# An encoder layer with neighbourhood attention and a gated scan: level scores on four column tiles in two runs per block, and second query copies by DMA

## The chip, the core and the metric

The kernel runs on one core of a Trainium2 chip. The metric is the device time of one execution in microseconds. Engine names are those of the profile: PE is TensorE (PEld its weight loads), DVE is VectorE, ACT is ScalarE, POOL is GpSimd and SP is SyncE; POOL and SP here mostly issue DMAs.

## What is computed

One encoder layer over 2048 tokens (a grid of 32 rows by 64 columns) with 1024 features, in float32. One input projection feeds an attention of 8 heads over a clamped 8 x 16 window with a learned bias, and a gated linear scan of 4 heads in both directions; both results are gated, concatenated, projected and normalised.

```python
h = jnp.einsum('btd,de->bte', x, w_in) + b_in
q_a, k_a, v_a, g_a, q_h, z_fwd, z_bwd, i_h, g_h = jnp.split(h, split_at, axis=-1)
o_a = neighbourhood_attention(heads_a(q_a), heads_a(k_a), heads_a(v_a), rpb) * jax.nn.silu(g_a)
# scan, per direction: S_t = diag(f_t) S_{t-1} + k_t outer v_t,  o_t = S_t^T q_t
o_fwd = hgrn2_chunk_scan(qh, k_f, ih, logf_f)
o_bwd = flip(hgrn2_chunk_scan(flip(qh), flip(k_b), flip(ih), flip(logf_b)))
o_h = rms_norm(o_fwd + o_bwd) * hg_norm_gain * jax.nn.silu(g_h)
y = jnp.einsum('bte,ed->btd', jnp.concatenate([o_a, o_h], axis=-1), w_out) + b_out
out = layer_norm(DEEPNORM_ALPHA * x + y)
```

## The kernel before, in words

Tokens are worked on in four blocks of 512, in two halves of two blocks. A half has four scan units (`hg_unit`, one head each) and four attention units (`att_unit`, two heads each). The input projection (`projections`) is written as a generator that issues one 128x512 matmul at a time: PE records `pj`, and `pv` for the two wide value projections. These are the **fillers**. Each unit is a generator as well, and yields weights; the driver at the end of `_build` spreads the fillers of a unit (between two entries of `marks`) over these weights. `in_order` (behind `mm` and `transpose`) ties TensorE's instructions to the order in which the code issues them, so TensorE's order is written by hand: unit work, some fillers, unit work. The other engines' instructions are ordered by a scheduler, roughly by the order of the code, with `tc.high_priority` moving some ahead. Float32 operands of the big projections are split into two float32r parts, a rounded one (a cast on ScalarE) and the rest (a subtraction on VectorE).

**A scan block** (`hg_phase1`, 16 in all: four heads, four token blocks) works by levels. In each chunk of 128 tokens it needs a 128x128 score matrix `A`. The diagonal comes from `ks` and `q`; the pairs at distance level 1, 2, 4, 8, 16, 32 each from a pair of mixed operands `km` and `qm` (in buffers named km, qm, ub or kt, copied by ScalarE at L502 and L504); level 64, the off-diagonal halves, from `ST` itself. Between levels VectorE multiplies running products into `ST` (L513, L514) and halves the products (`PX`, L516). The scores are held until the last level and then all issued in one run (`visit`, PE records `plev`): 64 matmuls with 64 output columns and 64 moving columns, which write the upper or lower 64 partitions of four PSUM banks. `collect` puts them together: a multiply by an identity (L481) and predicated copies with a mask per level (L483) into `AH`, which holds the two diagonal 64x64 blocks, then four copies into `A` (L485 to L488). Then follow the transposes `pk`, the state updates `pu` and `pub`, and the outputs `po`.

**An attention unit** goes through groups of 8 token rows; a group has four items, one per column window. `prep_q` splits a query tile for both heads into `hi` and `lo`, each of which is needed in both halves of the partitions: four casts on ScalarE and four subtractions on VectorE of 64x512 (L709 to L712). `prep_k` splits the keys into `KK`, 256 columns at a time (L726, L727). Per item `scores` issues four matmuls (PE `S`) and the softmax on VectorE and ScalarE, `turn` transposes the weights two items later (`ptr`), and `weigh` multiplies with the values (`pov`) for two items at a time and multiplies the gate in (L798); after the group's second `weigh` a DMA on POOL's queue stores the result in `cat`.

The scan's normalised outputs are gated later, in `deferred` calls of `hg_gate`. The end of the kernel (PE `yp`) is the output projection and the layer norm, which the change doesn't touch.

Of the kernel before, what the change touches and what calls it, by code (L numbers as in the profile page):

```python
# [18 lines left out]
P = 128  # L19
# [3 lines left out]
TB = 512  # L23
# [7 lines left out]
HC = 64  # L31
BUFS = dict(
    ST=3, PP=1, PX=1, ks=2, km=4, qm=4, A=2, kt=2, ub=6, op=6, AH=1, dec=6, Sf=1, Sb=1, ms=2,
# [43 lines left out]
def _build():  # L77
# [19 lines left out]
    with tile.TileContext(nc) as tc, ExitStack() as top:  # L97
# [24 lines left out]
        bv_sb = cp.tile([P, 4 * P], F32, name="bv_sb")  # L122

        def first_consts():
            make_identity(nc, ident)
            nc.sync.dma_start(out=b_sb, in_=b_in)
            nc.vector.tensor_scalar(out=bs_sb, in0=b_sb, scalar1=0.5, scalar2=None, op0=ALU.mult)
            nc.vector.tensor_scalar(out=b_sb[:, 0:4], in0=b_sb[:, 0:4], scalar1=0.125, scalar2=None, op0=ALU.mult)
            nc.sync.dma_start(out=gain_sb, in_=gain_in)
            nc.sync.dma_start(out=bv_sb, in_=bv_in)  # L130
# [181 lines left out]
        def projections():  # L312
# [31 lines left out]
            for m, job in enumerate(jobs):  # L344
# [36 lines left out]
                for i in range(4):  # L381
# [7 lines left out]
                    w = ws[key][i]  # L389
                    for t, ps in enumerate(banks):  # L390
# [9 lines left out]
                        if what == "v4":  # L400
                            nc.vector.tensor_tensor(out=st, in0=ps, in1=bv_sb, op=ALU.add)
# [30 lines left out]
        def hg_phase1(u, tb, h, st):  # L432
# [18 lines left out]
            AH = wk("AH", [P, 4, HC], F32)  # L451
# [15 lines left out]
            def visit():  # L467

                banks = [ps_tile("ms", "plev").rearrange("p (i c t) -> p i c t", i=2, c=4) for _ in range(4)]
                places = [banks[i // 2][:, i % 2] for i in range(8)]  # L470
                half_scores(places[-1])
                for (l, km, qm), pl in zip(held[:-1], places):
                    score(pl, km, qm)
                done = list(zip(held, places))
                held.clear()
                return done

            def collect(done):
                for (l, km, qm), pl in done:
                    if l is None:  # L480
                        nc.vector.tensor_tensor(out=AH, in0=pl, in1=idh.unsqueeze(1).to_broadcast([P, 4, HC]), op=ALU.mult)  # L481
                    elif km is not None:
                        nc.vector.copy_predicated(AH, masks[:, l].unsqueeze(1).to_broadcast([P, 4, HC]), pl)  # L483
                    else:
                        nc.scalar.copy(out=A[0:HC, :, HC:P], in_=pl[0:HC])  # L485
                        nc.scalar.copy(out=A[HC:P, :, 0:HC], in_=pl[HC:P])
                        nc.vector.tensor_copy(out=A[0:HC, :, 0:HC], in_=AH[0:HC])
                        nc.vector.tensor_copy(out=A[HC:P, :, HC:P], in_=AH[HC:P])  # L488

            held.append((None, ks, q))  # L490
# [3 lines left out]
            for l, B in enumerate(LEVELS):  # L494
# [11 lines left out]
                else:  # L506
                    held.append((l, None, None))
                done = visit() if B == HC else ()
# [102 lines left out]
        def hg_unit(half, u, h, ahead):  # L611
# [52 lines left out]
            for i, tb in enumerate((3, 2, 1, 0)):  # L664
                deferred.append([4.5 + 0.5 * i, lambda tb=tb: hg_gate(u, tb, rs[tb], h["g", tb])])
# [7 lines left out]
        def att_unit(half, u, h, ahead):  # L673
# [28 lines left out]
            def prep_q(g):  # L702
# [4 lines left out]
                for hd, own, other, tag in ((0, A, Bh, "km"), (1, Bh, A, "qm")):  # L707
                    hi, lo = wk(tag, [P, TB], F32R), wk(tag, [P, TB], F32R)
                    nc.scalar.copy(out=hi[own], in_=q[own])  # L709
                    nc.scalar.copy(out=hi[other], in_=q[own])  # L710
                    nc.vector.tensor_tensor(out=lo[own], in0=q[own], in1=hi[own].bitcast(F32), op=ALU.subtract)
                    nc.vector.tensor_tensor(out=lo[other], in0=q[own], in1=hi[own].bitcast(F32), op=ALU.subtract)  # L712
                    QS[g].append((hi, lo))

            def part(n, rc):
                if (n, rc) in srcs:
                    return srcs[n, rc]
                return h[n, rc // 2][:, (rc % 2) * 256:(rc % 2) * 256 + 256]

            def prep_k(rc):  # L720


                i = rc - rc0
                k = part("k", rc)
                for hd, own, other in ((0, A, Bh), (1, Bh, A)):
                    nc.scalar.copy(out=KK[hd][own, i], in_=k[own])  # L726
                    nc.vector.tensor_tensor(out=KK[hd][other, i], in0=k[own], in1=KK[hd][own, i].bitcast(F32), op=ALU.subtract)  # L727
# [60 lines left out]
            def weigh(j, g):  # L788

                po = ps_tile("ms", "pov")  # L790
                for b in range(2):
                    nch, n, i0 = len(GROUP_RC[g]), 4 * WIN_W[j + b], GROUP_RC[g][0] - rc0
                    PTs = state.pop((j + b, g))
                    for ch in range(nch):
                        for hd, hh in ((0, A), (1, Bh)):
                            mm(po[hh, b * P:(b + 1) * P], V[i0 + ch][0:n, j + b, hh], PTs[hd][0:n, ch], ch == 0, ch == nch - 1)
                gate = nat(h["g", g])[:, :, 16 * j:16 * j + 32]
                nc.vector.scalar_tensor_tensor(  # L798
                    out=gate, in0=po[:, 0:2 * P].rearrange("p (c r) -> p r c", r=8), scalar=b_sb[:, 8 + u:9 + u],
                    in1=gate, op0=ALU.add, op1=ALU.mult)  # L800
                if j == 2:
                    nc.gpsimd.dma_start(out=cat[u][g], in_=h["g", g])

            def prep(g):
                if g not in QS:
                    prep_q(g)
                    for rc in GROUP_RC[g]:
                        if rc not in ready:
                            ready.add(rc)
                            prep_k(rc)  # L810
# [4 lines left out]
            def main():  # L815
# [3 lines left out]
                for i in range(len(items) + 3):  # L819
                    if i < len(items):  # L820
                        prep(items[i][1])
                        scores(*items[i])
                        if i + 2 < len(items) and there(items[i + 2][1]):
                            prep(items[i + 2][1])
                    if ahead is not None and i >= len(items) - 1:
                        ahead()
                    yield 1
                    if 0 <= i - 2 < len(items):
# [5 lines left out]
                    yield 1  # L834
                    if 0 <= i - 4 and i % 2 == 0:
                        weigh(*items[i - 4])
                    yield 1
# [5 lines left out]
        def gate_consts():  # L843
# [21 lines left out]
            masks = cp.tile([P, len(LEVELS) - 1, HC], U8, name="masks")  # L865
            idh = cp.tile([P, HC], F32, name="idh")
            pi = wk("mx", [P, 1], I32)
            fi = wk("kt", [P, HC], I32)
            nc.gpsimd.iota(pi, pattern=[[0, 1]], base=0, channel_multiplier=1)
            nc.gpsimd.iota(fi, pattern=[[1, HC]], base=0, channel_multiplier=0)  # L870
            after_x(nc.vector.tensor_scalar(out=pi, in0=pi, scalar1=HC - 1, scalar2=None, op0=ALU.bitwise_and))
            after_x(nc.vector.tensor_scalar(out=fi, in0=fi, scalar1=HC - 1, scalar2=None, op0=ALU.bitwise_and))
            eqs = wk("Sf", [P, len(LEVELS), HC])
            for l in range(len(LEVELS)):
                sh = wk("A", [P, HC], I32)
                nc.vector.tensor_scalar(out=sh, in0=fi, scalar1=l, scalar2=None, op0=ALU.logical_shift_right)
                sp_ = wk("nm", [P, 1], I32)
                nc.vector.tensor_scalar(out=sp_, in0=pi, scalar1=l, scalar2=None, op0=ALU.logical_shift_right)
                shf = wk("op", [P, HC])
                nc.vector.tensor_copy(out=shf, in_=sh)  # L880
                pf = wk("mx", [P, 1])
                nc.vector.tensor_copy(out=pf, in_=sp_)
                nc.vector.tensor_scalar(out=eqs[:, l], in0=shf, scalar1=pf, scalar2=None, op0=ALU.is_equal)
            nc.vector.tensor_copy(out=idh, in_=eqs[:, 0])
            for l in range(len(LEVELS) - 1):
                nc.vector.tensor_tensor(out=masks[:, l], in0=eqs[:, l + 1], in1=eqs[:, l], op=ALU.subtract)
            return masks, idh, fa, fb, fn
# [75 lines left out]
        masks, idh, fa, fb, fn = gate_consts()  # L963
# [177 lines left out]
```

## Time and profile before

| | us |
|---|---|
| median of 3 runs | 1302.32 |
| lowest and highest | 1301.87, 1302.68 |
| profiled execution | 1301.28 |
| its span | 1299.5 |

The profile is one execution. The page gives the busy time of each engine, a picture of the span in 40 slices, the chain of work that ended last, and the costliest groups of instructions (line, engine, operation, what is written from what, partitions x elements, count; then busy us, mean ns of one, and idle time before). The trace answers more closely: the chain in order of time (start, us, engine and tile, count), the groups with shapes kept apart, the busy time of each engine in a stretch, and who waited for whom (us in total, times, longest). A float32 matmul of the program appears in the trace as two records, a float32r matmul or a transpose as one.

### The profile page before, as it was taken

What the parts mean: (1) busy time and instruction counts of PE and PEld (TensorE: products, weight loads), DVE (VectorE), ACT (ScalarE), POOL (GpSimd) and SP (SyncE); (2) the same over time, 40 slices, a digit from 0 to 9 for tenths busy, and PEclk for the clock granted to TensorE, in tenths of its full rate; (3) what the DMA queues carried; (4) which work ended last, traced back from release to release, by engine and by line L of the source; (5) the groups of instructions that cost most, each with busy time, mean ns of one, the idle gap of its engine ahead of it and who ended that gap; (6) DMA issues with size and microseconds to landing.
All of it is one profiled execution on the core that took longest, in us unless ns stands there. A gap on an engine that the chain in (4) does not pass through costs nothing.

```text
span 1299.5 us, 23159 instructions
## 1 busy us (share of the span) xinstructions
PE 1285.2 (99%) x8726; PEld 1081.8 (83%) x8726; DVE 875.2 (67%) x2076; ACT 669.8 (52%) x1424; POOL 110.0 (8%) x204
## 2 busy tenths in 40 slices
PE   9999999999999999999999999999999999999997
PEld 7888888888888888888888888888888887888886
DVE  5853666666454364754787769686586879689855
ACT  5533555545454464624655555575677779631000
POOL 0010000013120000011010101302000000000000
PEclk9999999999999999999999999999999999999999
DMA  7342212134353265243131313636545467465411
GB/s 229 110 133 90 83 67 84 58 116 143 119 159 117 75 198 169 68 156 131 44 130 44 122 58 117 187 115 208 164 131 180 150 203 263 133 223 203 163 40 65
DMA packets 98386, 170.38 MB, mean 131 GB/s; under 512 B 11425, under 2 KB 42913, under 8 KB 98273
## 3 DMA queue, kind: packets, MB, share of 16 engines
q1 hardware_dynamic: 85840, 131.26, 31.7%
q0 software_dynamic: 12288, 37.50, 8.4%
q8 instruction: 69, 1.13, 0.4%
q14 instruction: 45, 0.36, 0.1%
q10 hardware_dynamic: 144, 0.13, 0.0%
HBM read 131.36 MB, written 37.49 MB: 130 GB/s over the span
## 4 chain that ended last, share of the span: by engine, by line
PE 92%; DVE 3%; ACT 2%; DMA 2%; issue 1%; DVEq 0%; ACTq 0%
PE pj L142 47%; PE yp L142 12%; PE pv L142 12%; PE plev L142 4%; PE pov L142 4%; PE ptr L145 3%; PE S L142 3%; PE po L142 2%; PE pu L142 1%; PE pub L142 1%; PE pk L145 1%; PE pb L142 1%; DMA woraw<-in_w_out_dram 1%; DMA ST<-in_vecs_dram 0%; PE warm L142 0%
## 5 line engine op out<-in xcount | busy, mean ns | idle before, releaser
L142 PE MATMUL pj<-xt,wt 128*128 128x512 f32 x2688 | 658.3, 395 | 0.1
L142 PEld LDWEIGHTS pj<-xt,wt 128*128 128x128 f32 x2688 | 493.2, 188 | 100.0 <-issue 3.9
L142 PE MATMUL pv<-wv,xt 128*128 128x512 f32 x768 | 183.3, 393 | 1.2 <-DVE wv L158 1.2
L142 PEld LDWEIGHTS pv<-wv,xt 128*128 128x128 f32 x768 | 142.0, 188 | 30.7 <-DVE wv L158 1.8
L142 PE MATMUL yp<-wo,chi 128*128 128x512 f32 (+1 forms) x528 | 162.2, 386 | 0.2 <-ACT chi L941 0.2
L768 ACT ACTIVATE ub<-ub,nm 128x384 f32<-128x384 f32 (+2 forms) x128 | 78.7, 616 | 90.2 <-DVE nm L767 90.1
L158 DVE TENSOR_TENSOR wt<-wraw,wt 128x512 fp32r<-128x512 f32 (+1 forms) x108 | 68.6, 666 | 70.1 <-ACT wt L157 70.0
L142 PEld LDWEIGHTS yp<-wo,chi 128*128 128x128 f32 x528 | 98.0, 189 | 20.0 <-ACT chi L941 0.6
L513 DVE TENSOR_TENSOR ST<-ST,PX 128x512 f32<-128x512 f32 x96 | 66.0, 688 | 46.4 <-PE plev L142 21.0
L239 ACT ACTIVATE ht<-pj,bs_sb 128x512 f32<-128x512 f32 x64 | 43.9, 687 | 81.0 <-PE pj L142 80.7
L502 ACT COPY km<-ST 128x512 f32<-128x512 f32 x64 | 44.7, 698 | 75.3 <-DVE ST L514 40.3
L158 DVE TENSOR_TENSOR wv<-vraw,wv 128x512 fp32r<-128x512 f32 x64 | 41.6, 686 | 43.4 <-ACT wv L157 43.1
L157 ACT CAST wt<-wraw 128x512 fp32r<-128x512 f32 (+1 forms) x108 | 59.8, 604 | 18.7 <-PE pv L142 17.1
L514 DVE TENSOR_TENSOR ST<-ST,PX 128x512 f32<-128x512 f32 x96 | 65.6, 683 | 0.0
L784 ACT COPY op<-ptr 96x384 f32<-96x384 f32 (+3 forms) x128 | 60.8, 524 | 7.1 <-PE ptr L145 7.0
L145 PE MATMUL ptr<-ident,ub 128*128 128x128 f32 (+1 forms) x448 | 59.9, 273 | 1.3 <-DVE rg L798 0.8
L145 PEld LDWEIGHTS ptr<-ident,ub 128*128 128x128 f32 (+1 forms) x448 | 51.7, 133 | 11.3 <-DVE rg L798 1.0
L157 ACT CAST wv<-vraw 128x512 fp32r<-128x512 f32 x64 | 36.5, 617 | 35.3 <-PE pv L142 24.0
L770 DVE TENSOR_SCALAR ub<-ub,rs 128x384 f32<-128x384 f32 (+2 forms) x128 | 51.8, 420 | 2.7
L1042 ACT ACTIVATE va<-mv,eps 128x2 f32<-128x2 f32 (+1 forms) x9 | 2.7, 295 | 94.8 <-DVE mv L1039 94.8
L767 DVE CUSTOM_DVE_ANT_0 ub<-S,PX 128x384 f32<-128x384 f32 (+2 forms) x64 | 33.8, 562 | 22.4 <-PE S L142 21.4
L767 DVE CUSTOM_DVE_ANT_0 ub<-S,PP 128x384 f32<-128x384 f32 (+2 forms) x64 | 33.7, 562 | 21.1 <-PE S L142 21.0
(216 smaller groups left out, 1880.5 us busy)
## 6 DMA issues: line engine op xcount, KB each, us to landing
wraw<-in_w_in_dram SPq DMA_DIRECT2D x118, 256.0 KB, 3.1
vraw<-in_w_v_dram SPq DMA_DIRECT2D x64, 256.0 KB, 2.7
xraw<-in_xT_dram SPq DMA_DIRECT2D x32, 256.0 KB, 4.1
craw<-cat SPq DMA_DIRECT2D x32, 256.0 KB, 3.5
PP<-in_rpb_dram SPq DMA_DIRECT2D x16, 384.0 KB, 3.9
PX<-in_rpb_dram SPq DMA_DIRECT2D x16, 384.0 KB, 3.7
cat<-hu POOLq DMA_DIRECT2D x20, 256.0 KB, 2.9
vh<-hv POOLq DMA_DIRECT2D x16, 256.0 KB, 3.7
```

Of the source, the lines that this page charges most:

```text
L142: in_order(nc.tensor.matmul(out, lhsT=lhsT, rhs=rhs, start=start, stop=stop, **kw))
L145: in_order(nc.tensor.transpose(out=out, in_=in_, identity=ident))
L157: nc.scalar.copy(out=hi, in_=raw)
L158: last_split[0] = nc.vector.tensor_tensor(out=lo, in0=raw, in1=hi.bitcast(F32), op=ALU.subtract)
L239: nc.scalar.activation(t, ps, AF.Tanh, bias=bs_sb[:, c:c + 1], scale=0.5)
L502: nc.scalar.copy(out=km.rearrange("p (n h b) -> p n h b", h=2, b=B), in_=mix(ST, 0, 3, B, 0, TB))
L513: nc.vector.tensor_tensor(out=S1, in0=S1, in1=pr[:, :, :, 0].unsqueeze(3).to_broadcast([P, 2, m, B]), op=ALU.mult)
L514: nc.vector.tensor_tensor(out=S2, in0=S2, in1=pr[:, :, :, 1].unsqueeze(3).to_broadcast([P, 2, m, B]), op=ALU.mult)
L767: nc.vector.tensor_tensor_reduce(out=sb[:, 0:nk], in0=s[:, 0:nk], in1=bt[:, hd, 0:nk], scale=-1.0, scalar=3e38, op0=ALU.add, op1=ALU.min, ...
L768: nc.scalar.activation(sb[:, 0:nk], sb[:, 0:nk], AF.Exp, bias=nm, scale=-1.0, accum_out=sums[:, hd:hd + 1])
L770: nc.vector.tensor_scalar(out=sb[:, 0:nk], in0=sb[:, 0:nk], scalar1=rs[:, hd:hd + 1], scalar2=None, op0=ALU.mult)
L784: nc.scalar.copy(out=PT[0:n, 0:nch].rearrange("p a b -> p (a b)"), in_=pt[0:n, 0:nch * P])
```

## The change

**The scores.** `score` now makes blocks of 32x32 on four column tiles: 16 matmuls with 32 output columns and 32 moving columns per level, instead of 8 of 64x64. Levels 1 to 16 and the diagonal then lie in the four diagonal 32x32 blocks; level 32 takes its moving columns from the neighbouring block (`e ^ other`); the off-diagonal halves are 16 matmuls of 32x64. The scores come in two runs per block: the diagonal and levels 1, 2, 4 when level 4 is reached, the rest at the last level. `collect` puts the halves into `A` with one wide ScalarE copy and the others with predicated copies, the last of which (`put`) write 128x512 with two new masks, `mwide`.

**The attention.** `prep_q` makes each second copy with a DMA on POOL's queue, unless it is asked for `soon`; it is called three items ahead instead of two. `prep_k` takes two key tiles at a time where they lie side by side. `weigh` takes a whole group of four items at once. The weights of the yields stay the same in sum.

**Besides.** `place_v` runs at high priority; the bias of the value projection is loaded into a rotating tile when it is needed, four times, instead of once; `hg_gate` calls move to other weights; `ks` has one buffer instead of two, `op` eight instead of six.

```diff
-    ST=3, PP=1, PX=1, ks=2, km=4, qm=4, A=2, kt=2, ub=6, op=6, AH=1, dec=6, Sf=1, Sb=1, ms=2,
+    ST=3, PP=1, PX=1, ks=1, km=4, qm=4, A=2, kt=2, ub=6, op=8, AH=1, dec=6, Sf=1, Sb=1, ms=2,
...
             w = wp.tile([P, 2, 2, 4 * P], F32R, tag="w", name="wv")
-            for o, raw in enumerate(raws):
-                split(w[:, :, o], raw)
+            with tc.high_priority(offset=PRIO):
+                for o, raw in enumerate(raws):
+                    split(w[:, :, o], raw)
...
+                    if i == 3 and what == "v4":
+                        bias = h_tile("bv")
+                        nc.sync.dma_start(out=bias, in_=bv_in)
...
-            def score(pl, km, qm):
+            def score(pl, km, qm, other):
                 for c in range(4):
-                    for e in range(2):
-                        cs = slice(c * P + e * HC, c * P + e * HC + HC)
-                        mm(pl[e * HC:e * HC + HC, c], km[:, cs], qm[:, cs], True, True)
+                    for e in range(4):
+                        k, t = c * P + e * QC, c * P + (e ^ other) * QC
+                        mm(pl[e * QC:(e + 1) * QC, c], km[:, k:k + QC], qm[:, t:t + QC], True, True)
             def half_scores(pl):
                 for c in range(4):
-                    l_, r_ = slice(c * P, c * P + HC), slice(c * P + HC, (c + 1) * P)
-                    mm(pl[0:HC, c], ST[:, 0, l_], ST[:, 2, r_], True, True)
-                    mm(pl[HC:P, c], ST[:, 3, r_], ST[:, 1, l_], True, True)
+                    for e in range(4):
+                        k, t = c * P + e * QC, c * P + (HC if e < 2 else 0)
+                        mm(pl[e * QC:(e + 1) * QC, c], ST[:, 0 if e < 2 else 3, k:k + QC], ST[:, 2 if e < 2 else 1, t:t + HC], True, True)
...
-                        nc.scalar.copy(out=A[0:HC, :, HC:P], in_=pl[0:HC])
-                        nc.scalar.copy(out=A[HC:P, :, 0:HC], in_=pl[HC:P])
-                        nc.vector.tensor_copy(out=A[0:HC, :, 0:HC], in_=AH[0:HC])
-                        nc.vector.tensor_copy(out=A[HC:P, :, HC:P], in_=AH[HC:P])
+                        put(mwide[:, 1], pl)
+                if done[0][0] is None:
+                    put(mwide[:, 0], AQ)
...
-                done = visit() if B == HC else ()
+                done = visit(B == HC) if B in (4, HC) else ()
...
-                deferred.append([4.5 + 0.5 * i, lambda tb=tb: hg_gate(u, tb, rs[tb], h["g", tb])])
+                deferred.append([((4.5, 6.5, 6.9, 7.5) if ahead is None else (0.5, 2.5, 3.5, 5.5))[i], lambda tb=tb: hg_gate(u, tb, rs[tb], h["g", tb])])
...
                     nc.scalar.copy(out=hi[own], in_=q[own])
-                    nc.scalar.copy(out=hi[other], in_=q[own])
                     nc.vector.tensor_tensor(out=lo[own], in0=q[own], in1=hi[own].bitcast(F32), op=ALU.subtract)
-                    nc.vector.tensor_tensor(out=lo[other], in0=q[own], in1=hi[own].bitcast(F32), op=ALU.subtract)
+                    if soon:
+                        nc.scalar.copy(out=hi[other], in_=q[own])
+                        nc.vector.tensor_tensor(out=lo[other], in0=q[own], in1=hi[own].bitcast(F32), op=ALU.subtract)
+                    else:
+                        for t in (hi, lo):
+                            nc.gpsimd.dma_start(out=t[other], in_=t[own])
...
-                        prep(items[i][1])
+                        prep(items[i][1], True)
                         scores(*items[i])
-                        if i + 2 < len(items) and there(items[i + 2][1]):
-                            prep(items[i + 2][1])
+                        if i + 3 < len(items) and there(items[i + 3][1]):
+                            prep(items[i + 3][1])
...
+                    if i >= 6 and i % 4 == 2:
+                        weigh(groups[(i - 6) // 4])
```

How the built program's rows move is shown at three places. The first is PE at the third scan block, before. `pj` are fillers, `plev` the scores, `pk` the transposes that follow them.

```order
L142 MATMUL po<-Sf,ST 128x128 x3
L142 MATMUL pj<-xt,wt 128x512 x87
L142 MATMUL plev<-ST 64x64 x8
L142 MATMUL plev<-hp,ks 64x64 x8
L142 MATMUL plev<-qm,km 64x64 x32
L142 MATMUL plev<-ub 64x64 x8
L142 MATMUL plev<-kt 64x64 x8
L142 MATMUL pj<-xt,wt 128x512 x10
L145 MATMUL pk<-ident,ST 128x128 x8
```

The same stretch of PE in the changed kernel:

```order
L140 MATMUL po<-Sf,ST 128x128 x4
L140 MATMUL pj<-xt,wt 128x512 x51
L140 MATMUL plev<-hp,ks 32x32 x16
L140 MATMUL plev<-qm,km 32x32 x48
L140 MATMUL pj<-xt,wt 128x512 x39
L140 MATMUL plev<-ST 32x64 x16
L140 MATMUL plev<-qm,km 32x32 x16
L140 MATMUL plev<-ub 32x32 x16
L140 MATMUL plev<-kt 32x32 x16
L140 MATMUL pj<-xt,wt 128x512 x10
L143 MATMUL pk<-ident,ST 128x128 x8
```

One run of 64 matmuls has become two runs of 64, with 39 fillers between them; the fillers in all, and the 10 before `pk`, are as before.

The second place is PE at the end of an attention unit of the second half, before (`ptr` are transposes of the softmax weights, `pov` the sums weighted by them):

```order
L145 MATMUL ptr<-ident,ub 128x128 x6
L142 MATMUL pj<-xt,wt 128x512 x5
L142 MATMUL pov<-op,A 64x128 x4
L142 MATMUL pov<-op,ks 64x128 x2
L142 MATMUL pov<-op,A 64x128 x4
L142 MATMUL pov<-op,ks 64x128 x2
L142 MATMUL pj<-xt,wt 128x512 x10
L145 MATMUL ptr<-ident,ub 96x128 x6
L142 MATMUL pj<-xt,wt 128x512 x20
```

and the same group in the changed kernel:

```order
L143 MATMUL ptr<-ident,ub 96x128 x6
L140 MATMUL pj<-xt,wt 128x512 x15
L140 MATMUL pov<-op,A 64x128 x4
L140 MATMUL pov<-op,ks 64x128 x2
L140 MATMUL pov<-op,A 64x128 x4
L140 MATMUL pov<-op,ks 64x128 x2
L140 MATMUL pov<-op,A 64x128 x4
L140 MATMUL pov<-op,ks 64x128 x2
L140 MATMUL pov<-op,A 64x128 x4
L140 MATMUL pov<-op,ks 64x128 x2
L140 MATMUL pj<-xt,wt 128x512 x10
```

The first of the group's two runs has moved behind its last transposes, into one run with the second.

The third place is POOL's queue in the changed kernel, where the first attention unit of the second half goes over into the next (`cat` is the store of a group's result, `km` and `qm` the copies within the query tiles):

```order
L828 DMA cat_2_84<-hu 128x512
L735 DMA km<-km 64x512 x2
L735 DMA qm<-qm 64x512 x2
L735 DMA km<-km 64x512 x2
L735 DMA qm<-qm 64x512 x2
L828 DMA cat_3_85<-hu 128x512
L735 DMA km<-km 64x512
L735 DMA qm<-qm 64x512
```

Before, the `cat` rows stood there with nothing between them. The copies of the last group and of the next unit's first group now stand ahead of the last store, those of the next unit's second group behind it.

More of the change, by code (lines that the diff above doesn't have):

```diff
@@ L400, in projections @@
                         if what == "v4":
-                            nc.vector.tensor_tensor(out=st, in0=ps, in1=bv_sb, op=ALU.add)
+                            nc.vector.tensor_tensor(out=st, in0=ps, in1=bias, op=ALU.add)
                             nc.gpsimd.dma_start(out=vhg[tb][:, :, t], in_=st.rearrange("p (u e) -> p u e", u=HG_HEADS))
@@ new lines, in visit @@
+            def visit(last):
+                n = 4 * QC
+                places = [(ps, i) for ps in [ps_tile("ms", "plev") for _ in range(2 if last else 1)] for i in range(0, TB, n)]
+                done = []
+                if last:
+                    half = places[0][0][:, 0:2 * n].rearrange("p (c t) -> p c t", c=4)
+                    half_scores(half)
+                    done.append((None, half))
+                    del places[:2]
+                for (l, km, qm), (ps, i) in zip(held, places):
+                    pl = ps[:, i:i + n].rearrange("p (c t) -> p c t", c=4)
+                    score(pl, km, qm, int(l == QC_LEVEL))
+                    done.append((l, pl))
@@ L490, in hg_phase1, with put @@
-            held.append((None, ks, q))
+                if not done:
+                    return
+                Av = A.rearrange("p c (k t) -> p c k t", t=QC)
+                def put(mask, t):
+                    nc.vector.copy_predicated(Av, mask.unsqueeze(1).to_broadcast([P, 4, P]).rearrange("p c (k t) -> p c k t", t=QC), spread(t, QC))
+                for l, pl in done:
+                    if l is None:
+                        nc.scalar.copy(out=A.rearrange("p c (k t) -> p c k t", t=HC), in_=spread(pl, HC))
+                    elif l == "diagonal":
+                        nc.vector.tensor_tensor(out=AQ, in0=pl, in1=idq.unsqueeze(1).to_broadcast([P, 4, QC]), op=ALU.mult)
+                    elif l < QC_LEVEL:
+                        nc.vector.copy_predicated(AQ, masks[:, l].unsqueeze(1).to_broadcast([P, 4, QC]), pl)
+                    else:
+                        put(mwide[:, 1], pl)
@@ L786, in turn, with weigh, prep @@
                 state[j, g] = PTs
[L788 removed]
+            def weigh(g):
                 po = ps_tile("ms", "pov")
[L791 to L793 removed]
+                nch, i0 = len(GROUP_RC[g]), GROUP_RC[g][0] - rc0
+                for j in range(4):
+                    n = 4 * WIN_W[j]
+                    PTs = state.pop((j, g))
                     for ch in range(nch):
                         for hd, hh in ((0, A), (1, Bh)):
[L796 to L797 removed]
+                            mm(po[hh, j * P:(j + 1) * P], V[i0 + ch][0:n, j, hh], PTs[hd][0:n, ch], ch == 0, ch == nch - 1)
+                gate = nat(h["g", g])
                 nc.vector.scalar_tensor_tensor(
[L799 to L804, printed above, removed]
+                    out=gate, in0=po.rearrange("p (c r) -> p r c", r=8), scalar=b_sb[:, 8 + u:9 + u], in1=gate, op0=ALU.add, op1=ALU.mult)
+                nc.gpsimd.dma_start(out=cat[u][g], in_=h["g", g])
+            def prep(g, soon=False):
                 if g not in QS:
[L806 to L808 removed]
+                    prep_q(g, soon)
+                    for rc, n in runs:
+                        if rc not in ready and any(rc <= r < rc + n for r in GROUP_RC[g]):
                             ready.add(rc)
[L810 removed]
+                            prep_k(rc, n)
             def there(g):
@@ L833, in main @@
                         turn(*items[i - 2])
[L834 to L837, printed above, removed]
+                    yield 2
             return (lambda: prep(groups[0])), main
@@ L862, in gate_consts @@
             nc.vector.tensor_scalar(out=fn, in0=fb, scalar1=-1.0, scalar2=None, op0=ALU.mult)
[L865 to L866 removed]
+            masks = cp.tile([P, QC_LEVEL, QC], U8, name="masks")
+            mwide = cp.tile([P, 2, P], U8, name="mwide")
+            idq = cp.tile([P, QC], F32, name="idq")
             pi = wk("mx", [P, 1], I32)
[L868 removed]
+            fi = wk("kt", [P, P], I32)
@@ L869, in gate_consts @@
             nc.gpsimd.iota(pi, pattern=[[0, 1]], base=0, channel_multiplier=1)
[L870 to L876, printed above, removed]
+            nc.gpsimd.iota(fi, pattern=[[1, P]], base=0, channel_multiplier=0)
@@ L885, in gate_consts @@
-            for l in range(len(LEVELS) - 1):
-                nc.vector.tensor_tensor(out=masks[:, l], in0=eqs[:, l + 1], in1=eqs[:, l], op=ALU.subtract)
-            return masks, idh, fa, fb, fn
+                nc.vector.tensor_scalar(out=out, in0=shf, scalar1=pf, scalar2=None, op0=ALU.is_equal)
+            equal(idq, pq, 0, QC)
+            for l in range(QC_LEVEL):
+                low = idq if l == 0 else eqs[:, l % 2, 0:QC]
+                high = eqs[:, (l + 1) % 2, 0:QC]
+                equal(high, pq, l + 1, QC)
+                nc.vector.tensor_tensor(out=masks[:, l], in0=high, in1=low, op=ALU.subtract)
@@ L890, in _build @@
+            equal(eqs[:, 2], pi, QC_LEVEL, P)
+            equal(eqs[:, 3], pi, QC_LEVEL + 1, P)
+            nc.vector.tensor_copy(out=mwide[:, 0], in_=eqs[:, 2])
+            nc.vector.tensor_tensor(out=mwide[:, 1], in0=eqs[:, 3], in1=eqs[:, 2], op=ALU.subtract)
+            return masks, mwide, idq, fa, fb, fn
         gots = [{} for _ in todo]
@@ L962, in _build @@
         advance(144)
-        masks, idh, fa, fb, fn = gate_consts()
+        masks, mwide, idq, fa, fb, fn = gate_consts()
         advance(marks[0])
```

50 lines of the change are left out of this document (22 added, 28 removed).

## The prediction

> **What bounds the kernel now.** I read the page first: the span, the busy shares, the chain that ended last.
>
> ```profile
> span 1299.5 us, 23159 instructions
> PE 1285.2 (99%) x8726; PEld 1081.8 (83%) x8726; DVE 875.2 (67%) x2076; ACT 669.8 (52%) x1424; POOL 110.0 (8%) x204
> PEclk9999999999999999999999999999999999999999
> PE 92%; DVE 3%; ACT 2%; DMA 2%; issue 1%; DVEq 0%; ACTq 0%
> ```
>
> TensorE is busy for 99% of the span at its full granted clock, and 92% of the chain is its own work. VectorE has a third of the span free, ScalarE half. So an edit counts by what it does to TensorE's own instruction stream, or by a wait that it makes or removes there. Two more views say how much there is to win by removing waits: the stretches of the span, and who kept TensorE waiting.
>
> ```profile
> 84.00:860.00 776.00, 775.45 (x5778) 660.33 (x5777) 489.12 (x1118) 408.13 (x846) 86.28 (x157) 1.00 0.34 110
> 860.00:1140.00 280.00, 275.44 (x1879) 227.91 (x1879) 209.01 (x585) 202.60 (x474) 17.10 (x31) 1.00 0.55 177
> ...
> PE S L142 <- DVE ST L727: 1.2, 2, 0.9
> ...
> PE pv L142 <- DVE wv L158: 1.2, 1, 1.2
> PE ptr L145 <- DVE rg L798: 0.8, 1, 0.8
> PE S L142 <- DVE hu L605: 0.7, 1, 0.7
> ```
>
> The columns of the first two rows are the stretch, its length, then PE, PEld, DVE and ACT busy. From 84 us to 1140 us, where every changed line but the set-up lies, TensorE stands idle for 0.55 + 4.56 = 5.1 us. That is all that better ordering or lighter VectorE and ScalarE can give; more must come from shorter TensorE work.
>
> **The scores.** The chain around one block of the scan, and two runs of the attention's weighted sum (pov), which pairs 64-column matmuls in the same way but with 128 moving columns instead of 64:
>
> ```profile
> 84.46 3.88 PE plev L142 x128
> 88.34 2.95 PE pj L142 x12
> ...
> 390.17 1.46 PE pov L142 x24
> ...
> 905.96 1.90 PE pov L142 x32
> ...
> L142 PE MATMUL plev<-qm,km 128*64 128x64 f32 x1024 | 32.6, 222 | 0.0
> L142 PE MATMUL pov<-op,A x256: 270/273/323, 918.1 to 1147.3; 96*64 96x128 f32 x64, 128*64 128x128 f32 x64
> ...
> 949.75 0.28 PE L142 MATMUL pov<-op,A 128*64 128x128 f32 x2
> ```
>
> Each float32 matmul of the program stands twice in the trace (64 in a block's scores, 128 records; 12 in a pov run, 24 records). In the last row two pov records that last at least 270 ns each together span 0.28 us: they began within 0.01 us of each other and ran side by side, one on each half of the columns. So I count pairs. pov: 8 more records, 4 pairs, cost 1.90 - 1.46 = 0.44 us, 0.11 us a pair; the rest of a run of 12 pairs, 1.46 - 12 x 0.11 = 0.14 us, is the price of entering it. plev: (3.88 - 0.14) / 64 pairs = 58.4 ns a pair. From 128 to 64 moving columns a pair falls from 110 to 58.4 ns, 0.81 ns a column, with 6.8 ns that don't depend on it.
>
> After the change a block has 128 score matmuls, 256 records: 224 with 32 moving columns and 32 (the half scores) with 64, each on 32 of the array's columns. If four stand side by side as two do now, that is 56 rounds of 32 columns and 8 of 64. No row shows a 32-column tile, so a round is bounded from both sides. Below: half of today's pair, 29.2 ns. Above: every record costs what it costs now, 29.2 ns, a round 117 ns. I take the line through the two rows, 6.8 + 32 x 0.81 = 32.6 ns, since the rows nearest to it show cost going with moving columns and not with the number of tiles. The half scores stay at 58.4 ns. Then the block falls from 64 x 58.4 = 3.74 us to 56 x 32.6 + 8 x 58.4 = 2.29 us, by 1.44 us; for 16 blocks **-23.1 us** (the lower bound makes it -26.2 us). All of it is on the path.
>
> Entering and leaving such runs costs something too: the 0.14 us, and the slow first plain matmuls behind it. But the scores now come in two runs per block (16 more) and pov in one run per group instead of two (32 runs become 16). Runs are 48 before and after, so whatever a switch costs drops out: 0.
>
> [...]
>
> **Copies, splits and collection.** Per query tile two ScalarE casts and two VectorE subtractions become four DMAs of 128 KB on POOL's queue (64 in all; in the built order every group takes this way).
>
> ```profile
> L710 ACT CAST km<-hp x12: 617/618/622, 331.5 to 1104.6; 64x512 fp32r<-64x512 f32 x12
> L712 DVE TENSOR_TENSOR km<-hp,km x12: 684/685/689, 333.4 to 1111.0; 64x512 fp32r<-64x512 f32 x12
> ...
> L481 DVE TENSOR_TENSOR AH<-plev,idh 128x256 f32<-128x256 f32 x16 | 6.7, 416 | 0.0
> L483 DVE COPY_PREDICATED AH<-masks,plev 128x256 f32<-128x256 uint8 x96 | 42.8, 446 | 1.5
> L487 DVE COPY A<-AH 64x256 f32<-64x256 f32 x16 | 4.5, 281 | 0.1
> L488 DVE COPY A<-AH 64x256 f32<-64x256 f32 x16 | 4.7, 295 | 0.2
> L516 DVE TENSOR_TENSOR PX<-PP 128x512 f32<-128x512 f32 x16 | 10.9, 681 | 0.0
> L516 DVE TENSOR_TENSOR PX<-PX 128x128 f32<-128x128 f32 x16 | 4.5, 282 | 0.0
> ```
>
> ScalarE loses 32 x 0.62 = 20 us, VectorE 32 x 0.69 = 22 us. A block's collection goes from 0.42 + 6 x 0.45 + 0.28 + 0.30 = 3.7 us on VectorE to one multiply and five predicated copies of 128 elements plus two of 512; with the size law of L516 (0.28 and 0.68 us) and 0.03 us more for a predicated copy that is 0.28 + 5 x 0.31 + 2 x 0.71 = 3.3 us. The wider K splits and gate products save a few us more. Neither engine is on the path, so this is worth only what it removes of the waits above: the k splits came late (1.2 us), and place_v gets priority (1.2 us). Bounds 0 and -5.1 us; I take **-2 us**.
>
> What is late next? The copies:
>
> ```profile
> 940.25 0.62 ACT L709 CAST km<-rq 64x512 fp32r<-64x512 f32 x1
> ...
> 943.50 0.69 DVE L712 TENSOR_TENSOR qm<-rq,qm 64x512 fp32r<-64x512 f32 x1
> ...
> 952.09 0.51 PE L142 MATMUL S<-ST,km 128*128 128x384 f32 x2
> ...
> 380.02 0.58 POOL L251 DMA_DIRECT2D sq<-hp  x1 [14.84 <-ACT hp L229]
> ...
> op<-sop POOLq DMA_DIRECT2D x8, 256.0 KB, 6.4
> ...
> sk<-hp POOLq DMA_DIRECT2D x4, 128.0 KB, 2.0
> ...
> POOL cat L802 <- DVE hu L798: 148.7, 11, 23.1
> ```
>
> In this unit the preparation starts at 940.25 and the first scores at 952.09. Without the second copies the first parts are done at most 2 x 0.62 + 2 x 0.69 = 2.6 us after the start, at 942.9; four issues of 0.58 us make 945.2; no row shows a copy within SBUF, so landing is bounded by 2.0 us (a store of 128 KB) and 6.4 us (the slowest load on that queue): 947.2 to 951.6. Both ends are in time, the later barely. For later groups the look-ahead grows from two items to three. But POOL is in order, and it has stood up to 23 us behind a cat store that waits for VectorE; a copy behind such a store would come late.
>
> The second cover is that of the last level's products. The half scores release them, and the transposes (pk) need them.
>
> ```profile
> 299.98 3.88 PE plev L142 x128
> 303.86 2.04 PE pj L142 x8
> ...
> 300.64 0.69 DVE L513 TENSOR_TENSOR ST<-ST,PX 128x512 f32<-128x512 f32 x1
> 301.25 0.69 DVE L514 TENSOR_TENSOR ST<-ST,PX 128x512 f32<-128x512 f32 x1
> ```
>
> The half scores end at 299.98 + 0.14 + 8 x 0.058 = 300.6; the products end at 301.94. Behind them TensorE now has 56 pairs, 3.3 us, before it turns to pj; after the change 24 rounds, 0.8 us. The second run would end near 301.4 and the pj matmuls add about 2 us: pk at 303.4, with 1.5 us to spare. So it is covered unless VectorE is busy elsewhere just then. For all new waits together (copies, pk, the earlier first run) I put **+1 us**; bounds 0 and, below, +12 us.
>
> Loading the v bias four times instead of once moves 0.75 MB more of 170 MB and costs nothing that TensorE sees; later hg_gate calls move transposes among fillers, 0.
>
> **Sum.** The profiled execution took 1301.28 us (span 1299.5 and 1.8 around it). 1301.3 - 23.1 - 2 + 1 = 1277.2 us. The median shown, 1302.32, is 1.0 us above that execution: **1278 us**, 1.9% faster.
>
> **The rivals.**
> - Narrow rounds don't run four wide: a round of four costs what a pair costs now, 58.4 ns. For: no row shows a 32-column tile. Against: cost goes with moving columns in both rows at hand. The gain of the scores is gone: 1302.3 - 1 = 1301 us.
> - Slower: TensorE takes each record at a fixed rate, the 29.2 ns that it takes on average now. The number of records doubles, from 128 to 256 a block, so this decides as soon as a record costs over 3.74 / 256 = 14.6 ns. At 29.2 ns a block loses 3.74 us, in all 60 us: 1361 us. For: twice the instructions, and a rate that the rows at hand never exceed over a whole run. Against: the starts within 0.01 us, and pov's cost, which follows the columns. [...]
> - New waits: copies caught behind a cat store hold the first scores of the four second-half units for 3 us each (the mean wait of POOL for such a store is 148.7 / 11 = 13.5 us, the slack about 10 us), or pk waits. +12 us: 1290 us.
> - The change doesn't do what it says: not here; the built order has all 64 copies, both runs and the 32-wide matmuls.
>
> **How the numbers follow.** Forecast 68% (1271 to 1284), new waits 14% (1284 to 1294), no gain 7%, fixed rate 10%, anything else 1%. The range leaves out the last three: 1270 (the lower round and all 5.1 us of waits gone) to 1292. Within 0.2%, 2.6 us, a measurement of this kernel can hardly tell a change from none: faster 0.83, same 0.07, slower 0.10.
>
> **What would show it.** plev on the chain near 2.6 us per block in two pieces, and its records' busy mean near 9 ns (a round over four); pov in 16 pieces. Wrong if plev's chain time grows above 3.88 us a block, if S waits for a POOL DMA, or if pk waits for L514's successor. If plev shrinks as said but the time does not, the gain went into those waits.

## The result, and the profile after

| | before | after |
|---|---|---|
| median, us | 1302.11 (4 runs) | 1278.8 (4 runs, 1277.9 to 1279.72) |
| profiled execution, us | 1301.28 | 1278.99 |
| ratio of the times | | 0.982, 95% interval 0.9803 to 0.9837 |

The changed kernel is 23.3 us faster, 1.8%. First the page: span, PE, and the shares of the chain.

```profile
span 1277.2 us, 27174 instructions
PE 1262.6 (99%) x10774; PEld 1063.1 (83%) x10774; DVE 841.1 (66%) x1984; ACT 642.4 (50%) x1344; POOL 143.1 (11%) x268
...
PE 93%; DVE 3%; DMA 2%; ACT 1%; issue 1%; SPq 0%; DVEq 0%; ACTq 0%
```

PE has 2048 records more and is busy for 22.6 us less, still 99% of the span. The stretches that answer to the two of before (stretch, length, PE, PEld, DVE, ACT, POOL busy, clock, DMA share, GB/s):

```profile
84.00:838.00 754.00, 753.79 (x7682) 636.65 (x7680) 471.84 (x1068) 391.16 (x791) 95.54 (x175) 1.00 0.37 116
838.00:1118.00 280.00, 275.71 (x1907) 234.92 (x1906) 192.29 (x536) 189.82 (x445) 41.82 (x79) 1.00 0.71 206
```

The bounds are chosen: both second stretches are 280 us long, and the first stretch is 22 us shorter after the change. They don't hold quite the same work, so the place of the gain is better read from the starts of two PE records that have the same other work ahead of them in both kernels. The last `pu`, behind the last scan block, starts 16.7 us earlier than before (841.2 and 824.5), and the first `yp` 21.9 us earlier (1081.0 and 1059.1): some 17 us are gained up to the end of the scan, some 5 us in the attention behind it. PE's idle time in the two stretches is 0.21 + 4.29 = 4.5 us, where it was 5.1. Over the whole span (span less PE's busy time) it is 14.6 us, where it was 14.3: the gain is shorter PE work, not shorter waits. Who kept PE waiting (us in total, times, longest):

```profile
PE pov L140 <- ACT op L811: 1.3, 1, 1.3
PE warm L140 <- DVE eps L1067: 1.2, 1, 1.2
PE ptr L143 <- DVE rs L796: 1.1, 1, 1.1
PE S L140 <- DVE nm L794: 0.9, 1, 0.9
PE ptr L143 <- ACT op L811: 0.8, 2, 0.5
PE pj L140 <- ACT xt L155: 0.6, 1, 0.6
PE plev L140 <- issue: 0.2, 1, 0.2
```

The waits of S for the K splits and of pv for wv are gone; others of the same size stand in their place (that of `warm`, 1.2 us, was there before as well). One scan block on the chain, answering to the 3.88 us in one piece of before (start, us, what), and VectorE's last products at the same place:

```profile
287.57 1.28 PE plev L140 x84
288.85 5.21 PE pv L140 x22
294.06 1.81 PE pj L140 x8
295.87 1.44 PE plev L140 x95
297.31 2.04 PE pj L140 x8
299.35 0.87 PE pk L143 x8
```

```profile
297.13 0.68 DVE L533 TENSOR_TENSOR ST<-ST,PX 128x512 f32<-128x512 f32 x1
```

The scores take 1.28 + 1.44 = 2.7 us in two pieces. The products end at 297.81, pk begins at 299.35: 1.5 us to spare. For the length of a round the page is too coarse; here are the times from each start of a record to the fourth start after it, in ns, in a first run (from 73.15 us) and in the half scores at the head of a second run (from 85.99 us):

```
52 32 32 31 32 32 31 32 | 42 49 33 33 34 33 33 35 | 43 48 34 34 33 33 33 35 | 43 49 33 32 34 33 33
80 56 56 56 55 56 56 56
```

A round of four takes 32 ns, one of half scores 56 ns. Where a new level begins (the bars) two rounds together take some 25 ns more, and with these the mean behind the first round is 35.5 ns. What these 25 ns are was not tried.

Last the copies, in an attention unit of the second half. The preparation on the timeline (start, us, engine, line, what):

```profile
920.57 0.63 ACT L728 CAST km<-rq 64x512 fp32r<-64x512 f32 x1
...
923.16 1.02 POOL L735 DMA_DIRECT2D qm<-qm  x2
```

The view of the DMAs (queue, count, KB each, median us from issue to landing):

```profile
km<-km POOLq DMA_DIRECT2D x32, 128.0 KB, 4.1
qm<-qm POOLq DMA_DIRECT2D x32, 128.0 KB, 4.1
```

And the unit's first scores on the chain:

```profile
931.97 0.71 PE S L140 x4
```

The last copy is issued by 924.2. At the median of 4.1 us it lands at 928.3 at the latest, and the trace has its landing at 926.6. The chain's row of the scores begins at 931.97, their first record at 931.81.

### The profile page after: what moved, and what is told of

The parts are those of the page before. It is cut to its first block, busy times and chain, and to the rows that moved or that the text cites. A ratio compares the mean times of both kernels' runs of the same rounds, so it can differ in the third digit from the quotient of the medians.

```text
span 1277.2 us, 27174 instructions
## 1 busy us (share of the span) xinstructions
PE 1262.6 (99%) x10774; PEld 1063.1 (83%) x10774; DVE 841.1 (66%) x1984; ACT 642.4 (50%) x1344; POOL 143.1 (11%) x268
## 4 chain that ended last, share of the span: by engine, by line
PE 93%; DVE 3%; DMA 2%; ACT 1%; issue 1%; SPq 0%; DVEq 0%; ACTq 0%
PE pj L140 47%; PE yp L140 13%; PE pv L140 13%; PE pov L140 4%; PE ptr L143 4%; PE plev L140 3%; PE S L140 3%; PE po L140 2%; PE pk L143 1%; PE pub L140 1%; PE pu L140 1%; DMA craw<-cat 1%; PE pb L140 1%; PE pt L143 1%; DVE ST L754 1%
## 5 line engine op out<-in xcount | busy, mean ns | idle before, releaser
L140 PEld LDWEIGHTS pv<-wv,xt 128*128 128x128 f32 x768 | 141.9, 188 | 28.7 <-issue 0.2
```

What stands on the lines that cost most here:

```text
L140: in_order(nc.tensor.matmul(out, lhsT=lhsT, rhs=rhs, start=start, stop=stop, **kw))
```

## The experiments

The theory: the scores' four-wide rounds are the whole gain, each run of side-by-side matmuls has a price, and the rest of the change moves little. The rivals were that switches are free, and that the lighter ScalarE and VectorE carry part of it.

**The scores alone** on the kernel before: `score`, `half_scores`, `visit`, `collect` and the masks of after, all else of before.

> The kernel before with the scores part alone: four column tiles, two runs a block, their masks and collection; the weighted sum stays in two runs a group, the copies and splits stay on ScalarE and VectorE. My theory: the scores are the whole gain and every run of side-by-side matmuls costs about 0.35 us to enter and leave. The traces of before and after give 4.08 us for a block's one run and 2 x 1.54 = 3.08 us for its two, beyond the plain matmuls beside them: 16 x 1.00 = 16.0 us less, 1302.1 - 16 = 1286 us (1283 to 1288). Rival 1, the prediction's sum with free switches: 1302.1 - 23.1 = 1279 us. Rival 2, the lighter ScalarE and VectorE of the other parts carry the gain: above 1292 us.

Measured: 1288.41 us, ratio to before 0.9894 (0.9878 to 0.9911), in this group 13.4 us less than before. That is between the two, and just outside my bounds. In its trace the 896 rounds take 35.4 ns on average, starts of levels and runs included, instead of the prediction's 32.6, which gives 2.5 us of the 23.1 back. If all of the rest is the price of the 16 further runs, they have cost 23.1 - 2.5 - 13.4 = 7.2 us, 0.45 us each (0.41 by PE's busy time, which falls by 14.0 us; PE also stands idle 1.3 us longer here than before). By this remainder switches aren't free, and rival 2 falls. The next run gives their price without the prediction's sum.

**The weighted sum in two runs** a group, on the kernel after, with `weigh` itself as before:

```diff
-                    if i >= 6 and i % 4 == 2:
-                        weigh(groups[(i - 6) // 4])
+                    if i >= 4 and i % 2 == 0:
+                        weigh(*items[i - 4])
```

> The changed kernel with the weighted sum in two runs a group again (16 runs more, the same matmuls). My theory, a price per run: the traces give 1.66 and 2.11 us for the two runs of before and 2.97 and 3.67 us for the one run of after, in all 7 us: 1278.8 + 7 = 1286 us (1283 to 1288). Rival, runs cost nothing and the merging only removed waits or nothing: 1278 to 1280 us.

Measured: 1285.93 us, 0.9873 (0.9858 to 0.9888). 16 runs more with the same matmuls cost 7.1 us, 0.44 us each (0.39 by PE's busy time, 1268.8 us against 1262.6): the same price as above from another tile, and the theory's number.

**The copies by the engines**: `if soon:` becomes `if True:`, so that ScalarE and VectorE make every second copy.

> The changed kernel with the queries' second copies made by ScalarE and VectorE again, for every group; the 64 DMAs are gone. My theory: hidden either way, 1278.8 us within 1.5. Rival 1: the DMA copies took 20 us from ScalarE and 22 us from VectorE that counted somewhere: 1281 us or more. Rival 2: the DMAs slow TensorE's loads or hold POOL: under 1277 us.

Measured: 1279.12 us, 0.9824 (0.9809 to 0.9838): no difference to after. The second of the two parts that the title names, the queries' copies by DMA, is hidden either way.

**Three ordering edits undone** (`place_v` without priority, `hg_gate` at the old weights, look-ahead of two):

> The changed kernel with three ordering edits undone: place_v's splits without priority, the gate products called at 4.5, 5.0, 5.5 and 6.0, the look-ahead of the preparation two items instead of three. The prediction gave 2 us to removed waits (to which these edits belong) and took 1 us for new ones. My theory: waits of about one us are moved about and not removed: 1278.8 us within 1.5. Rival: 1280 to 1282 us, with the wait of pv for wv and of S for the K splits back in the list of waits.

Measured: 1279.2 us, 0.9823 (0.981 to 0.9837). No difference, and neither pv nor the K splits came back into the list of waits; its longest, of pov for op, is 1.8 us here and 1.3 after.

**One run per block**, since a run costs some 0.4 us: `visit` once, at level 64, with three banks.

```diff
-                places = [(ps, i) for ps in [ps_tile("ms", "plev") for _ in range(2 if last else 1)] for i in range(0, TB, n)]
+                places = [(ps, i) for ps in [ps_tile("ms", "plev") for _ in range(3)] for i in range(0, TB, n)]
...
-                done = visit(B == HC) if B in (4, HC) else ()
+                done = visit(True) if B == HC else ()
```

> The changed kernel with a block's scores in one run of 256 records on four column tiles, instead of two of 128. My theory: 16 runs fewer at 0.35 us: 1278.8 - 5.6 = 1273 us. Rival 1, a run costs nothing: 1279 us. Rival 2, the first run was put early for a reason: the collection's VectorE work comes in one piece behind the single run and the transposes of the last products, or po, wait for it, 0.3 to 1 us a block: 1279 to 1290 us.

Measured: 1326.45 us, 1.0182 (1.0167 to 1.0197): 47.6 us slower than after, and slower than the kernel before. No theory had this. The longest entry in its list of waits of PE:

```profile
PE plev L140 <- issue: 32.1, 15, 3.6
```

Its chain around the first block:

```profile
84.15 2.55 PE plev L140 x163
86.70 3.60 issue
90.30 0.26 PE plev L140 x3
```

Its stretches from the stop on (columns as above):

```profile
86.50:90.30 3.80, 0.20 (x24) 0.09 (x11) 2.35 (x6) 0.99 (x2) 0.56 (x1) 1.00 0.61 235
90.30:94.30 4.00, 4.00 (x14) 3.13 (x14) 3.71 (x10) 1.27 (x2) 0.00 (x0) 0.58 0.02 6
```

Its span and mean granted clock, which is 0.999 after:

```profile
core 0: 1325.2 us, clock 0.982
```

In 15 of 16 blocks PE stops in the middle of the scores, for nothing that the profile shows, and behind the first stop the granted clock is 0.58 for 4 us (such a drop follows 11 of the 15 stops). The two together make the loss: 32.1 + 1.2 us of waits for issue, some (0.999 - 0.982) x 1278 = 22 us of clock, less 7 us for the 16 runs that are gone, is 48 us. Why it stops is in the places. Here is the number of the first PE record behind each stop (the program's first record is 0), and the step from one to the next in units of 127 records:

```
record  606  988  1369  1878  2259  2641  3022  3404  4930  5439  5945  6326  6704  7592  7974
step      -  3.0   3.0   4.0   3.0   3.0   3.0   3.0  12.0   4.0   4.0   3.0   3.0   7.0   3.0
```

All steps are whole numbers, to the decimal shown. The page's DMA queues (packets, MB, share) have one that brings instructions:

```profile
q8 instruction: 85, 1.39, 0.5%
```

It brings 85 pieces of 16 KB; 10774 records and as many weight loads are 2 x 10774 / 85 = 253 a piece, 127 records of load and matmul. So PE stops where one piece of its instructions ends and the next isn't there. Around the first stop that queue's packets begin at 82.16, 87.96 and 91.89 us; the stop ends at 90.30. It is so at all 15: a packet of that queue begins 2.2 to 3.1 us before the stop ends, though the 85 packets come some 16 us apart on average. Other transfers don't explain it: in the stops that end at 173.53, 639.42 and 721.99 us the DMA share is 0.00. Every stop lies at the 142nd to 252nd record of its run, so at least the second such border in it; the border before it, 127 records or 1.2 us earlier, was passed without a stop. At the pace of the fillers (0.227 us from start to start on the median, in the trace of after) a piece lasts 127 x 0.227 = 29 us. The sixteenth block stops at another border of this row, record 7213, four steps behind 6704 and four records behind the block's run: that is the wait of 1.2 us. How many pieces lie ready ahead is not shown; what these stops show is that PE passed one border of a run at this pace, and not the second.

**Two runs of 192 and 64** test the length against the place of the run and the banks that it takes: `if B in (16, HC)`, and `range(2)` banks in both.

> The changed kernel with a block's scores in two runs of 192 and 64 records (the first one two levels later) instead of 128 and 128; same matmuls, same number of runs. My theory for the one-run kernel's loss: TensorE's instructions come in pieces of 16 KB by the queue that the page calls instruction, a four-wide run takes 256 records in 2.2 us, and what lies ready runs out after 142 to 252 records; then TensorE waits 0.4 to 3.8 us for the next piece, and the granted clock drops behind it. A run of 192 then runs dry in about half the blocks: 8 to 20 us slower, 1287 to 1299 us, all of it as waits of plev for issue in the long runs. Rival, the single run lost because of where it stood or of the banks that it took: both runs here take two banks and the second stands where it did: 1278 to 1281 us.

Measured: 1302.6 us, 1.0013 (1.0002 to 1.0024), 23.8 us slower than after; the sign and the mechanism of the theory, and 4 us more than its upper end. Its longest waits of PE:

```profile
PE plev L140 <- issue: 15.5, 7, 2.4
PE pv L140 <- issue: 2.5, 1, 2.5
```

Its chain at the first block:

```profile
78.29 1.49 PE plev L140 x96
79.78 2.35 issue
82.12 0.58 PE plev L140 x39
```

Its span and clock:

```profile
core 0: 1300.5 us, clock 0.994
```

Stops in 7 of 16 long runs, none in the short ones, at records 479, 1370, 3408, 4935, 5824, 6712 and 7092: again 127 times a whole number apart (7, 16, 12, 7, 7, 3). The wait of pv is one more of these, at record 3026, directly behind a long run. The borders that lie between the stops follow from those that show. With them two borders fall into every run of 256 records and into 10 of the 16 runs of 192. Where the second is at the 142nd record of the run or later, PE stops at it (22 runs in the two kernels); where it is at the 130th to 140th, it doesn't (4 runs). So in these runs about one piece was worked off at this pace without a stop. Waits of 18 us and (0.999 - 0.994) x 1283 = 6 us of clock make the 24 us; I had not added the clock.

**What sets a round** was tried with narrower moving operands. On the kernel after:

```diff
-                        mm(pl[e * QC:(e + 1) * QC, c], km[:, k:k + QC], qm[:, t:t + QC], True, True)
+                        mm(pl[e * QC:(e + 1) * QC, c, 0:16], km[:, k:k + QC], qm[:, t:t + 16], True, True)
```

> The changed kernel with 16 moving columns instead of 32 in every score matmul except the half scores (the other half of each score tile is left out; the collection reads the computed half twice, same sizes). Rival, the prediction's line of 6.8 + 0.81 ns a moving column: a round falls from 32 to about 20 ns, 896 rounds lose 11 us: 1268 us. My theory: a round is not set by moving columns alone; loading a weight tile of 32 columns takes as long, so narrower moving gains nothing: 1278.8 us within 1.5, rounds stay at 31 to 33 ns.

And on the kernel before:

```diff
-                        mm(pl[e * HC:e * HC + HC, c], km[:, cs], qm[:, cs], True, True)
+                        mm(pl[e * HC:e * HC + HC, c, 0:32], km[:, cs], qm[:, c * P + e * HC:c * P + e * HC + 32], True, True)
```

> The kernel before (two column tiles of 64) with 32 moving columns instead of 64 in its score matmuls, half scores apart (half of each score tile is left out; the collection reads the computed half twice). Rival, the prediction's line in moving columns: a pair falls from 58.4 to 32.6 ns, 896 pairs lose 23 us: 1279 us. My theory, the width of the loaded weights sets it: pairs stay at 58 ns, 1302 us within 2.

Measured: 1277.76 us, 0.9812 (0.9799 to 0.9826), and 1303.48 us, 1.001 (1.0001 to 1.0018). Neither gains anything near its rival's 11 and 23 us. In the groups, the row of the mixed levels after:

```profile
L140 PE MATMUL plev<-qm,km 128*32 128x32 f32 x2048 | 24.6, 199 | 0.0
```

The same with 16 moving columns:

```profile
L140 PE MATMUL plev<-qm,km 128*32 128x16 f32 x2048 | 23.9, 185 | 0.0
```

And before with 32 moving columns, where the row has 32.6 us with 64:

```profile
L142 PE MATMUL plev<-qm,km 128*64 128x32 f32 x1024 | 32.6, 223 | 0.0
```

By the distances of the starts, too, rounds stay at 32 to 33 ns and pairs at 58 ns. Halving the moving columns alone does nothing. Nor does halving the weight tile alone: the half scores after, 64 moving columns on tiles of 32, take 56 ns a round. Only where both sides are 32 or less is it 32 ns. That leaves a plain rate of 8 ns a record as a rival for the 32 ns.

**Two tiles at a time**: the matmuls of a level in another order, same results.

```diff
-                for c in range(4):
-                    for e in range(4):
+                for c, e in [(c, e) for p in (0, 2) for c in range(4) for e in (p, p + 1)]:
+                    if True:
```

> The changed kernel with the score matmuls of a level (half scores apart) in another order: first all those of column tiles 0 and 1 in turn, then all those of 2 and 3; the same matmuls and results. My theory: a tile of 32 columns can take the next record only 32 ns after the last, and four tiles do this side by side. With two in turn a level of 32 records takes 16 x 32 ns instead of 8 x 32: 896 x 32 ns = 28.7 us more, 1307 us (1303 to 1310). Rival: what the 16-column run met was a rate of about 8 ns a record, whichever tile it goes to: 1279 us, unchanged.

Measured: 1285.47 us, 0.9872 (0.9855 to 0.9888): 6.7 us more than after, which neither had. The timeline at the border of two levels says why:

```profile
86.77 0.43 PE L140 MATMUL plev<-qm,km 128*32 128x32 f32 x22
87.01 0.22 PE L140 MATMUL plev<-ub 128*32 128x32 f32 x2
87.03 0.23 PE L140 MATMUL plev<-qm,km 128*32 128x32 f32 x3
87.06 0.20 PE L140 MATMUL plev<-ub 128*32 128x32 f32 x1
```

Matmuls of the next level (ub) start ahead of the last ones of this level (qm,km), though the program issues them behind: by its order the first matmuls of a level are on tiles 0 and 1 and its last on tiles 2 and 3, so those on tiles 0 and 1 overtake those that stand in line for tiles 2 and 3. So four tiles are busy for much of the time even in this order. At the end of a run, where no next level follows, the starts are, in most runs, 25 and 6 or 7 ns apart in turn, and in all of them two records take 32 ns, on two tiles. That bears the theory out (a tile takes a record each 32 ns, and the four tiles do so side by side), and the plain rate of 8 ns falls; the 28.7 us did not come since PE didn't keep the order.

**The same order in one run**, meant to slow the pace at which instructions are taken:

> The one-run kernel (a block's 256 score records in one run) with that same order, two column tiles in turn: the run takes its instructions at about half the pace, some 4.1 us instead of 2.3 us of work. The comparison is with the two-run kernel in this order, about 1307 us. My theory, instructions run out: the pieces come in the same time as before, so most of the wait is now covered by work: 16 runs fewer take 6 us off, what is left of the waits is 0 to 1.5 us a block: 1301 to 1325 us. Rival, the loss is of the place of the run or its three banks: 32 us of waits and the lower clock come back in full, 1307 + 48 = 1355 us.

Measured: 1324.17 us, 1.0167 (1.0149 to 1.0186), inside my range, but it tells nothing of what it was made for: the order above hardly slowed the pace, so the waits stayed in the list:

```profile
PE plev L140 <- issue: 29.0, 14, 3.1
```

What it gives is another thing: its stops stand at the same 15 record numbers as those of the one-run kernel, one by one, although they end up to 4.4 us earlier. They go by the place in the program.

No version that computes everything beats the changed one. A run of 256 would save 7 us of switches and loses far more; the runs of 128, hardly longer than a piece of 127, stopped once in 32, for 0.2 us by the list of waits.

## Why the prediction was right

The time came out at 1278.8 for a forecast of 1278.0. Step by step:

- **TensorE bounds the kernel, other engines' work doesn't count.** Right. DVE lost 34 us of work and ACT 27 us, and giving the copies' share of it (some 21 us on DVE, 20 us on ACT) back cost nothing.
- **Four-wide rounds.** Right in kind, and nearly in size: 32 ns in the steady state for 32.6, 35.4 with the starts of levels and runs, 2.5 us less gain in all. But the line by which the number was found, 0.81 ns per moving column, was wrong as a law: with moving columns halved alone, pairs stay at 58 ns and rounds at 32 ns. That it gave the right number is luck: it held because the change narrows the weight tile with the moving operand. pov's 128 moving columns against 64 weight columns (110 ns) and the half scores after (64 against 32, 56 ns a round) go with the moving columns; the wider of the two sides sets the round, as far as these six shapes show.
- **Run switches cancel.** Right, by two prices: 16 runs more of scores at 0.45 us (a remainder), 16 fewer of pov at 0.44 us (measured). The 0.14 us of entry was a part of that price only. Behind a run of scores the step from the first filler to the second is 0.34 us, before and after, where 0.227 us is the median.
- **Waits, -2 + 1.** Not borne out. In the two stretches PE's idle time falls by 0.6 us (5.1 to 4.5), but over the whole span it grows by 0.3 us (14.3 to 14.6); the prediction took the stretches for the place of every changed line, but the first scores now start at 73.15 us, and its own pov row ran on to 1147.3. The waits named did go, but the ordering edits are worth nothing that can be measured, and new waits came elsewhere.
- **Copies and pk covered.** Right: the copies shown land at least 3.5 us ahead of their scores, no wait of S for a copy stands in the list, pk had the 1.5 us to spare that were worked out.
- **The sum.** The two runs that try the parts give 13.4 us for the scores and 7.1 us for the merged weighted sum, 20.5 us. PE's busy time fell by 22.6 us from before to after; some 2 us of it were not traced. The wider K splits, the gate products and the buffers had no run of their own. That the forecast came so close is in part luck: it had 2.6 us too much for rounds and runs and 1.3 us too much for waits, and these 2 us, which it didn't have, made up for half.
- **The rival of a fixed rate**, 29.2 ns a record, falls: starts on different tiles are 6 to 7 ns apart, and over a round of four, too, it is 32 ns, 8 ns a record.
- **What it did not see.** It treated the split into two runs as a matter of switches. The split is what makes the gain possible: with the same matmuls in one run the change would have been 1.8% slower than before. A rival "instructions run out" was missing, and the page shows what it takes: the instruction queue's 85 pieces, and a run's records against a piece's 127.

## What to carry to other kernels

In this kernel the time of narrow matmuls side by side on column tiles went with the wider of weight tile and moving operand (a round took 32 ns where the wider was 32, and 56 to 58 ns where it was 64), and each run of them cost some 0.4 us to enter and leave, so they should come in few runs; but none of these should cross two borders of the 16 KB pieces in which its instructions arrive, here 127 records of load and matmul each, at some 9 ns a record. Before merging runs, divide the records by the packets of the instruction queue; a wait for "issue" in the middle of a run, at steps of that number, is its sign. When a number falls out of a line through two rows, ask which other size changed along with it between them, and try the one alone.

## What the runs showed of the hardware that was not expected

- Instructions ran out: the stops of up to 3.8 us, start to start, came in 15 of 16 runs of 256 records, in 7 of 16 of 192 and in 1 of 32 of 128. The drop of the clock behind them (to 0.58 for 4 us behind the first) cost two thirds as much again, by the estimate above (22 us beside 33 us of waits).
- Matmuls on different column tiles started out of program order: with two tiles in turn, the first ones of the next level started at 87.01 us, and ones of the level before still at 87.03. Starts on different tiles were 6 to 7 ns apart, on one tile of 32 columns 32 ns.
